# A two-layer hybrid trunk on one core: inputs in one transfer, products of zeros in front, first block ordered by kind, sums and last transfers moved

## The chip, the core and the metric

The kernel runs on one core of a Trainium2 chip. The core has five engines with queues of their own: TensorE (PE, matrix products; its weight loads are listed apart as PEld), VectorE (DVE), ScalarE (ACT), GpSimd (POOL) and SyncE (SP, which here issues the transfers from the chip's memory). The metric is the device time of one execution in microseconds (us); lower is better.

## What is computed

Two layers, each a mixer and a convolutional feed-forward block (FFN), with six modulation vectors made from a conditioning vector `c`, and a norm at the end. Everything is float32, 256 tokens of 1024 channels.

```
def reference(x, c, positions, mod_w, mod_b, norm1_g, norm2_g, w_in, ...):
    for l in range(DEPTH):                      # DEPTH = 2
        mod = c @ mod_w[l] + mod_b[l]
        sh1, sc1, g1, sh2, sc2, g2 = [m[:, None, :] for m in jnp.split(mod, 6, axis=-1)]
        h = _rmsnorm(x, norm1_g[l]) * (1.0 + sc1) + sh1
        x = x + g1 * _mixer(h, positions, w_in[l], ...)
        h = _rmsnorm(x, norm2_g[l]) * (1.0 + sc2) + sh2
        x = x + g2 * _conv_ffn(h, w_up[l], conv_w[l], conv_b[l], w_down[l])
    return _rmsnorm(x, final_g)
```

`_mixer` projects `h` by one wide matrix, runs a sparse attention (an indexer picks 64 keys) and a forgetting attention (a cumulative bias), gates both and projects back. `_conv_ffn` is an up-projection to 2 x 2816 columns, a three-tap convolution along the tokens, `silu(a) * b`, and a down-projection.

## The kernel before, in words

**Tiling.** `x` is kept transposed in SBUF: 8 blocks of 128 channels by 256 tokens (`KT = 8`). Weights come from memory in chunks of about 128 x 1024 float32 into a ring (`raw`). Each chunk is split into a high part `whi` (made by ACT) and a low part `wlo` (made by DVE, raw minus high), activations likewise into `hh`, `hl`; a product is made of three passes: high by high, high by low, low by high (`mm3`, line 121).

**What sets the order.** The program is a list of steps (`add`, line 133), run in order by `run_steps` (line 141); each step names the chunks it needs, and the loader issues their transfers on SP in the order in which the steps list them, as ring slots come free. A scheduler then orders the instructions of each engine by a cost model, except for engines that are pinned (`pin`, line 74): those keep the order in which the code was written.

**The start.** Five transfers are issued first: positions, frequencies, 80 columns of small vectors, and `x` in two halves (lines 244 to 250). `begin` squares `x` and adds the squares; `tables` makes the rotary sines and cosines on DVE and ACT; `masks` makes the masks. `go0` (line 642) then makes the first block of the scale and shift of layer 0 as matrix products of `c` (padded in `cpad`) with a pair of chunks (`mod_mm`, line 615: psM<-raw,cpad), sums the squares over the channels by products with a column of ones (`sum_rows`: psC<-ones), takes the root on POOL (`rstd`), spreads it (psC<-ident,rstd), turns the block's modulation (`mod_fin`: psM<-ident,mods) and makes the block of `h` (`ht` on DVE, `hh` on ACT, `hl` on DVE).

**The blocks.** `go` (line 654) runs over the 8 blocks of channels. Block k multiplies block k of `h` by a 1096-column chunk `wrow[k]` into the accumulators (psA, psB), while the modulation for block k+1 is finished; the modulation products of block k+2 stand at its end, those of block 1 ahead of block 0. A block's modulation is one pair of chunks.

**The other modulation vectors.** They are made on DVE: one chunk of `wmodT` times `c`, summed along the row, one instruction for 128 values (line 357; in the profile CUSTOM_DVE_ANT_0 raw<-raw,cB,vc). There are 80, spread over the stages by the lists `MIXV` and `FFNV` (lines 43, 44): 24 in the mixer of layer 0, 32 in the FFN of layer 0, 16 in the mixer of layer 1, 8 in the FFN of layer 1. In an FFN, `PACE` says how early they are done: all by 1/1.3 of the stage.

**Between stages.** Each norm needs the sum of squares over all channels: squares on ACT, added up on DVE (`sqacc`) or summed one by one on PE. While the root is made, PE runs products whose results nobody reads (`warm`, psM<-cum), in numbers given by `WARMS`. `DSUM = 4` says that at an FFN's end the first four squares are added on DVE. `first_ups` (line 1008) runs the first three up-projections of an FFN block by block as `h` is made.

**The end.** `last` (line 1094) ends the down-projection; the result, scaled by the final gain, is turned back to token rows on PE (psB<-ident,x and psA<-ident,x), multiplied by the root (`yout`), and written out in four transfers of 256 KB on SP (line 1159).

## Time and profile before

| | us |
|---|---|
| median of 3 timed runs | 808.23 (806.09 to 808.28) |
| the profiled execution | 800.14 |
| its span, first to last instruction | 798.3 |
| PE busy in it | 774.5 (97%) |
| DVE busy | 671.2 (84%) |
| ACT busy | 486.8 (61%) |
| mean granted TensorE clock | 0.993 |

The profile is one execution. It was 8.09 us faster than the median of the timed runs; 1.84 us of its time lie outside its span. Rows that begin with two times are from the timeline: start, duration, engine, line, operation, output<-input, shapes, and how many instructions were merged (x8); brackets give the idle time of the engine ahead of it and what ended it. All recorded operations go through one helper, so that every engine shows line L88; the names of the tiles tell them apart. Records of a float32 product with ones or with `cpad` come in twos for each instruction of the program.

### The profile page before, as it was taken

The numbers are of one execution on the slowest core, as the hardware profiler recorded it, in microseconds if no ns is written. First come the engines' busy times: TensorE is split into PE (matmuls) and PEld (weight loads), VectorE is DVE, ScalarE is ACT, GpSimd is POOL, SyncE is SP. The second block draws the span as 40 slices with busy tenths as digits, with TensorE's granted clock in tenths as the row PEclk, the third lists the DMA queues.
The fourth block names the chain that finished last, engine by engine and source line by source line (L and its number), as shares of the span: only waits on it lengthen the run. The fifth ranks groups of instructions, "written<-read, shape, count | busy, mean of one in ns | idle before, by whom it ended". The sixth has DMA issues, their size and how long they took to land.

```text
span 798.3 us, 16595 instructions
## 1 busy us (share of the span) xinstructions
PE 774.5 (97%) x6419; PEld 749.7 (94%) x6419; DVE 671.2 (84%) x1441; ACT 486.8 (61%) x888; POOL 8.0 (1%) x21
## 2 busy tenths in 40 slices
PE   4999999999999999999999999999999999999996
PEld 2899989989999999999989999999999999999996
DVE  6689999998589999998776899997858887877764
ACT  4476566655386665667555756675538666666664
POOL 2000000000000000000000000000000000000000
PEclk9999999999999999999999999999999999999998
DMA  8956777888558999977534577784755766556501
GB/s 324 407 177 204 259 231 255 281 291 289 191 161 285 331 337 334 330 243 225 170 120 122 161 249 248 245 283 150 240 195 156 257 218 211 188 185 186 185 27 54
DMA packets 51919, 179.74 MB, mean 225 GB/s; under 512 B 6272, under 2 KB 6400, under 8 KB 51840
## 3 DMA queue, kind: packets, MB, share of 16 engines
q1 hardware_dynamic: 51840, 178.68, 66.5%
q8 instruction: 50, 0.82, 0.4%
q14 instruction: 29, 0.24, 0.1%
HBM read 177.61 MB, written 1.05 MB: 224 GB/s over the span
## 4 chain that ended last, share of the span: by engine, by line
PE 62%; issue 26%; DVE 8%; ACT 3%; DMA 1%; SPq 0%; POOLq 0%; POOL 0%; DVEq 0%; ACTq 0%
PE psA L88 39%; PE psB L88 19%; DVE wlo L88 2%; PE psM L88 2%; DVE sc L88 1%; PE psC L88 1%; DVE raw L88 1%; ACT whi L88 1%; DMA raw<-wqkf 1%; DMA x<-xT 1%; DVE lg L88 1%; DVE m L88 0%; ACT sq L88 0%; ACT y L88 0%; DVE x L88 0%
## 5 line engine op out<-in xcount | busy, mean ns | idle before, releaser
L88 ACT ACTIVATE whi<-raw 128x1024 fp32r<-128x1024 f32 (+3 forms) x252 | 254.3, 1013 | 140.8 <-PE psA L88 55.8
L88 DVE TENSOR_TENSOR wlo<-raw,whi 128x1024 fp32r<-128x1024 f32 (+3 forms) x252 | 292.1, 1165 | 56.3 <-ACT whi L88 55.4
L88 PE MATMUL psB<-hl,whi 128*128 128x256 f32 x768 | 212.9, 279 | 0.5 <-DVE hl L88 0.5
L88 PE MATMUL psB<-hh,whi 128*128 128x256 f32 x768 | 212.8, 279 | 0.0
L88 PE MATMUL psB<-hh,wlo 128*128 128x256 f32 x768 | 212.6, 278 | 0.0
L88 PEld LDWEIGHTS psB<-hl,whi 128*128 128x128 f32 x768 | 143.7, 188 | 1.0 <-DVE hl L88 0.9
L88 PEld LDWEIGHTS psB<-hh,wlo 128*128 128x128 f32 x768 | 144.0, 188 | 0.0
L88 PEld LDWEIGHTS psB<-hh,whi 128*128 128x128 f32 x768 | 143.6, 188 | 0.2
L88 PE MATMUL psA<-hh,whi 128*128 128x256 f32 x448 | 127.7, 286 | 0.1
L88 PE MATMUL psA<-hl,whi 128*128 128x256 f32 x448 | 125.3, 280 | 0.0
L88 PE MATMUL psA<-hh,wlo 128*128 128x256 f32 x448 | 125.0, 280 | 0.0
L88 DVE CUSTOM_DVE_ANT_0 raw<-raw,cB,vc 128x1024 f32<-128x1024 f32 x80 | 101.6, 1272 | 0.5 <-DMA raw<-wmodT 0.5
L88 PE MATMUL psA<-gl,whi 128*128 128x256 f32 x352 | 97.7, 278 | 0.0
L88 PE MATMUL psA<-gh,whi 128*128 128x256 f32 x352 | 97.4, 279 | 0.3
L88 PE MATMUL psA<-gh,wlo 128*128 128x256 f32 x352 | 97.6, 278 | 0.0
L88 PEld LDWEIGHTS psA<-hh,whi 128*128 128x128 f32 x448 | 84.0, 188 | 2.2 <-issue 1.7
L88 PEld LDWEIGHTS psA<-hl,whi 128*128 128x128 f32 x448 | 84.2, 188 | 0.4
L88 PEld LDWEIGHTS psA<-hh,wlo 128*128 128x128 f32 x448 | 84.1, 188 | 0.0
L88 DVE SCALAR_TENSOR_TENSOR y<-us,vc,y 128x255 f32<-128x255 f32 (+1 forms) x176 | 76.1, 477 | 3.8 <-ACT y L88 3.7
L88 PEld LDWEIGHTS psA<-gh,whi 128*128 128x128 f32 x352 | 65.7, 188 | 0.7 <-ACT gh L88 0.7
L88 PEld LDWEIGHTS psA<-gh,wlo 128*128 128x128 f32 x352 | 66.2, 188 | 0.0
L88 PEld LDWEIGHTS psA<-gl,whi 128*128 128x128 f32 x352 | 66.0, 188 | 0.0
(202 smaller groups left out, 1173.5 us busy)
## 6 DMA issues: line engine op xcount, KB each, us to landing
raw<-wup SPq DMA_DIRECT2D x88, 512.0 KB, 4.3
raw<-wmodT SPq DMA_DIRECT2D x80, 512.0 KB, 4.9
raw<-wdn SPq DMA_DIRECT2D x44, 512.0 KB, 3.9
raw<-wgate SPq DMA_DIRECT2D x32, 512.0 KB, 4.5
raw<-wrow SPq DMA_DIRECT2D x16, 548.0 KB, 6.5
raw<-wbr SPq DMA_DIRECT2D x16, 512.0 KB, 4.8
raw<-wout SPq DMA_DIRECT2D x16, 512.0 KB, 4.0
raw<-wqa SPq DMA_DIRECT2D x16, 320.0 KB, 2.9
```

The costliest lines, as they stand in the source:

```text
L88: r = fn(*a, **kw)
```

## The change

1. **Inputs.** Positions, frequencies and the small vectors are put in front of `x` in one array, and come with it in two transfers on SP (`xs`, 560 KB and 512 KB); `x` becomes a view of it. The zeroing of `tri`, `causal`, `chunked`, `LF` and `cum` goes from DVE to POOL. `cpad` and `vc` get their values by copies on POOL, behind the zeroing of the eight key tiles.
2. **Products of zeros.** `begin` issues 20 products of `cum` (zeros then) on PE; 4 and 10 more stand in `go0`.
3. **First block.** The two sums of squares are no longer added on DVE: PE sums each. `tables` is cut into five steps (`angles`, `turns`, `wholes`, `clamp`, `tables`) which stand with `masks` behind blocks 1 to 6. Block 0 is ordered by kind (all high by high products, then the modulation products of block 1, then all low by high, then all high by low). Chunks are requested one block later, so that `wrow[1]` comes ahead of the modulation pair of block 2.
4. **Sums moved.** The first four sums of vector 3 of layer 1 go from the mixer of layer 1 to the FFN of layer 0 (36 there, 12 in the mixer); `PACE` is 1.15; the mixer's remaining sums begin one step later (`MSTART`).
5. **FFN start.** The gains are made ahead of the last residual instead of behind it; in `first_ups` the further splits of weights begin at block 4 instead of block 1.
6. **Between the FFN of layer 0 and the mixer of layer 1** 3 products without use go ahead of the sums (0 before), and 9 instead of 8 behind them.
7. **The end.** `DSUM` is 2 in layer 1; the sums by products with ones go ahead of the turns, those of blocks 0 to 3 ahead of the last six products. The result leaves in three transfers: 512 KB on SP, 256 KB on ACT's queue, 256 KB on SP.

The diff, cut to its core:

```diff
-WARMS = {"ffn": (4, 8, 10), "mixer": (0, 8, 7)}
+WARMS = {"ffn": (4, 8, 10), "mixer": (3, 9, 7)}
-MIXV = (((0, 2), (0, 3), (0, 4)), ((1, 3), (1, 4)))
-FFNV = (((0, 5), (1, 0), (1, 1), (1, 2)), ((1, 5),))
+MIXV = (((0, 2), (0, 3), (0, 4)), ((1, 3, 4, 8), (1, 4)))
+FFNV = (((0, 5), (1, 0), (1, 1), (1, 2), (1, 3, 0, 4)), ((1, 5),))
-PACE = 1.3
+PACE = 1.15
-DSUM = 4
+DSUM = (4, 2)
+MSTART = (0, 1)
...
-    nc.sync.dma_start(posi, pos)
-    nc.sync.dma_start(ivf, invf)
-    nc.sync.dma_start(vc[:, :V_L + V_CW], vec[:, :V_L + V_CW])
-    for i in range(2):
-        nc.sync.dma_start(x[:, 4 * i:4 * i + 4, :], xT[:, 4 * i:4 * i + 4, :])
+    half = NS + KT * T // 2
+    nc.sync.dma_start(xs[:, :half], xT[:, :half])
+    nc.sync.dma_start(xs[:, half:], xT[:, half:])
...
-    V.memset(f(cum), 0.0)
+    G.memset(f(cum), 0.0)
...
+    def warm(n):
+        for _ in range(n):
+            PE.matmul(HD["fox"][1][:, 0, :], cum[:, :P], cum, start=True, stop=True, skip_group_check=True)
     def begin():
+        pin("V", "PE")
+        clear_keys()
+        HD["fox"] = [halves(bank("B")) for _ in range(2)]
+        HD["sp"] = bank("C")
+        warm(20)
         sq = work.tile([P, 2, 4, T], F32, name="sq0", tag="hl")
+        V.tensor_scalar(ident, jp, 0.0, None, op0=OP.is_equal)
+        G.tensor_copy(cpad[:, :, 0], xs[:, V_C:V_C + KT])
+        G.tensor_copy(vc[:, :V_L + V_CW], xs[:, :V_L + V_CW])
...
-        a, b = ACC["s"]
-        V.tensor_add(a, a, b)
...
             def go0(a, b):
                 pin("V", "A", "PE")
-                start()
+                sum_rows(HD["sp"], ACC["s"][0], True, False)
                 mod_mm(0, 0, a)
-                sp = bank("C")
-                sum_rows(sp, ACC["s"][0], True, True)
+                sum_rows(HD["sp"], ACC["s"][1], False, True)
+                r = rstd(HD["sp"])
                 mod_mm(0, 1, b)
-                r = rstd(sp)
                 state["split_hi"](1)
+                warm(4)
                 mod_fin(0, r)
+                warm(10)
+                start()
...
+            def first(w, a, b):
+                products(w, 0)
+                state["split_hi"](2)
+                mod_both(1, a, b)
+                products(w, 1)
+                state["split"](2)
+                mod_fin(1)
+                products(w, 2)
             def go(k, w, *mc):
-                if k == 0:
-                    mod_both(1, *mc[:2])
-                    mc = mc[2:]
...
+                mod_both(k + 1, *mc)
                 state["split_hi"](2)
...
-                if mc:
-                    mod_both(k + 2, *mc)
             for k in range(KT):
...
+                for fn in {1: [angles], 2: [turns], 3: [wholes], 4: [clamp], 5: [tables], 6: [masks]}.get(k, ()):
+                    add(fn, ahead=0)
...
         def merge(n, w):
             if n == KT - 1:
                 pin(*PINL)
+                gains(l, V_N2, 32)
...
-                if k == 1:
+                if k == 4:
                     state["split"](4)
...
+                if l + 1 == L:
+                    if b == 2:
+                        sum_rows(S["sp"], ACC["a"], True, False)
+                        pin("A", "PE")
+                    while sq and sq[0][0] < 2 * b:
+                        sums(False)
+                    while b < 3 and S["turn"] and S["turn"][0] < 2 * b:
+                        to_rows()
...
+            A.activation(y[:, 0, c], S["tok"][i][0], AF.Copy, scale=r[:, 0:1])
+            V.tensor_scalar(y[:, 1, c], S["tok"][i][1], r[:, 1:2], None, op0=OP.mult)
+            if i == 0:
+                nc.sync.dma_start(rows[:, :, c], y[:, :, c])
+            else:
+                nc.scalar.dma_start(rows[:, 0, c], y[:, 0, c])
+                nc.sync.dma_start(rows[:, 1, c], y[:, 1, c])
```

How the instructions move, as the built programs list them (line, operation, output<-input, shape, and how often in a row). First PE at the program's start, before:

```order
L88 MATMUL psM<-raw_126,cpad 32x256 x4
L88 MATMUL psC<-ones,sqh 128x1 x2
L88 MATMUL psM<-raw_128,cpad 32x256 x4
L88 MATMUL psM<-ident,mods 128x128 x2
L88 MATMUL psC<-ident,rstd 128x128 x2
L88 MATMUL psM<-raw_132,cpad 32x256 x4
L88 MATMUL psM<-raw_134,cpad 32x256 x4
L88 MATMUL psA<-whi,hh 128x320
L88 MATMUL psA<-whi,hh 128x264
L88 MATMUL psA<-whi,hl 128x320
```

The same place on PE, after the change:

```order
L93 MATMUL psB<-cum 128x256 x20
L93 MATMUL psC<-ones,sqh 128x1 x2
L93 MATMUL psM<-raw_119,cpad 32x256 x4
L93 MATMUL psC<-ones,sqh 128x1 x2
L93 MATMUL psM<-raw_121,cpad 32x256 x4
L93 MATMUL psB<-cum 128x256 x4
L93 MATMUL psM<-ident,mods 128x128 x2
L93 MATMUL psC<-ident,rstd 128x128 x2
L93 MATMUL psB<-cum 128x256 x10
L93 MATMUL psA<-whi,hh 128x320
L93 MATMUL psA<-whi,hh 128x264
```

34 products of `cum` are added, the sums of squares now stand on both sides of the first half of the modulation products, and the pair for block 1 (raw_132, raw_134) has left the place ahead of block 0. Next ACT at the start, before:

```order
L88 ACT_TABLE_LOAD
L88 ACTIVATE sq_145<-x 128x1024 x2
L88 ACT_TABLE_LOAD
L88 ACTIVATE ss<-ang 128x2x8
L88 ACTIVATE cc<-nt 128x2x8
L88 COPY mods<-psM 128x256
L88 ACTIVATE whi<-raw 128x1096
L88 ACTIVATE hh<-ht,mod_124 128x256
L88 COPY mods<-psM 128x256
L88 ACTIVATE whi<-raw 128x1096
```

ACT at the start, after the change:

```order
L93 ACT_TABLE_LOAD
L93 ACTIVATE sq_171<-xs 128x1024 x2
L93 COPY mods<-psM 128x256
L93 ACTIVATE whi<-raw 128x1096
L93 ACTIVATE hh<-ht,mod_117 128x256
L93 ACTIVATE whi<-raw 128x1096
L93 COPY mods<-psM 128x256
L93 ACTIVATE hh<-ht,mod_117 128x256
```

The second table load and the sine and cosine have left (they stand five blocks later), and the high part of the second weight chunk (the second `whi`) now stands ahead of the second copy of `mods`. Last, PE at the program's end, before:

```order
L88 MATMUL psA<-gh,wlo 128x256
L88 MATMUL psC<-ones,sqacc 128x1 x2
L88 MATMUL psB<-ident,x 128x128 x2
L88 MATMUL psC<-ones,sq 128x1 x2
L88 MATMUL psA<-ident,x 128x128 x2
L88 MATMUL psC<-ones,sq 128x1 x4
L88 MATMUL psA<-ident,x 128x128 x2
L88 MATMUL psC<-ones,sq 128x1 x2
L88 MATMUL psA<-ident,x 128x128 x4
```

And PE at the end, after the change:

```order
L93 MATMUL psC<-ones,sqacc 128x1 x2
L93 MATMUL psC<-ones,sq 128x1 x4
L93 MATMUL psB<-ident,xs 128x128 x4
L93 MATMUL psA<-gh,whi 128x256
L93 MATMUL psA<-gl,whi 128x256
L93 MATMUL psA<-gh,wlo 128x256
L93 MATMUL psA<-gh,whi 128x256
L93 MATMUL psA<-gl,whi 128x256
L93 MATMUL psA<-gh,wlo 128x256
L93 MATMUL psC<-ones,sq 128x1 x8
L93 MATMUL psA<-ident,xs 128x128 x8
```

Three sums and two turns now stand ahead of the last six products of the down-projection, and the other four sums stand ahead of the last turns instead of between them.

## Rows read from the trace of the kernel before

**Rows 1.** Windows: us, busy us and count by engine, PEclk, DMA share, GB/s.

```profile
0.00:10.00 10.00, 0.58 (x8) 0.23 (x8) 8.40 (x39) 4.40 (x4) 4.55 (x16) 1.00 0.69 235
10.00:20.00 10.00, 8.26 (x53) 5.31 (x46) 5.12 (x19) 3.99 (x8) 0.69 (x1) 1.00 1.03 413
...
240.00:360.00 120.00, 120.00 (x1061) 120.00 (x1060) 120.00 (x195) 76.39 (x115) 0.00 (x0) 1.00 0.89 310
...
400.00:410.00 10.00, 8.23 (x55) 7.82 (x54) 5.08 (x15) 5.02 (x10) 0.69 (x1) 0.83 0.11 44
450.00:540.00 90.00, 89.58 (x697) 84.06 (x696) 88.89 (x280) 59.17 (x144) 0.00 (x0) 1.00 0.74 245
620.00:760.00 140.00, 140.00 (x1191) 140.00 (x1190) 108.97 (x168) 89.18 (x133) 0.00 (x0) 1.00 0.63 203
```

**Rows 2.** Timeline of the start: start us, duration us, engine, what.

```profile
0.74 0.38 SPq L245 DMA_DIRECT2D posi<-pos  x1
...
2.11 0.91 SPq L250 DMA_DIRECT2D x<-xT  x2
...
7.92 1.06 ACT L88 ACTIVATE sq<-x 128x1024 f32<-128x1024 f32 x1 [0.23 <-DMA x<-xT]
...
9.00 1.28 ACT L88 ACT_TABLE_LOAD   x1
...
11.75 1.01 PE L88 MATMUL psC<-ones,sqh 128*128 128x1 f32 x4 [1.25 <-DVE sqh L88]
...
12.70 1.08 PE L88 MATMUL psM<-raw,cpad 128*32 128x256 f32 x8
...
15.74 1.94 PE L88 MATMUL psM<-raw,cpad 128*32 128x256 f32 x16
...
17.60 0.86 PE L88 MATMUL psA<-whi,hh 128*128 128x320 f32 x2
...
18.45 1.12 ACT L88 ACTIVATE whi<-raw 128x1096 fp32r<-128x1096 f32 x1 [0.34 <-DMA raw<-wrow]
...
19.83 0.17 DVE L88 TENSOR_REDUCE modr<-psM 128x2 f32<-128x8 f32 x1 [1.23 <-PE psM L88]
...
20.94 0.51 ACT L88 ACTIVATE hh<-ht,mod 128x256 fp32r<-128x256 f32 x1 [1.37 <-DVE ht L88]
...
21.93 1.07 PE L88 MATMUL psM<-rawg,cpad 128*32 128x256 f32 x16
...
22.93 0.54 PE L88 MATMUL psA<-whi,hh 128*128 128x320 f32 x2
...
27.37 0.54 PE L88 MATMUL psA<-whi,hh 128*128 128x320 f32 x2
```

**Rows 3.** Page, costliest groups: what, count | busy, mean ns | idle before.

```profile
L88 DVE TENSOR_TENSOR wlo<-raw,whi 128x1024 fp32r<-128x1024 f32 (+3 forms) x252 | 292.1, 1165 | 56.3 <-ACT whi L88 55.4
...
L88 DVE CUSTOM_DVE_ANT_0 raw<-raw,cB,vc 128x1024 f32<-128x1024 f32 x80 | 101.6, 1272 | 0.5 <-DMA raw<-wmodT 0.5
```

**Rows 4.** Timeline between the first FFN and the second mixer, PE.

```profile
402.40 0.61 PE L88 MATMUL psC<-ones,sqacc 128*128 128x1 f32 x4 [1.53 <-DVE sqacc L88]
...
405.06 1.92 PE L88 MATMUL psM<-cum 128*128 128x256 f32 x8
```

**Rows 5.** Timeline of the end.

```profile
787.82 1.65 DVE L88 SCALAR_TENSOR_TENSOR x<-psA,mod,x 128x256 f32<-128x256 f32 x4
...
791.92 0.69 POOL L390 TENSOR_TENSOR rstd<-var,mhalf 128x2 f32<-128x2 f32 x1 [195.13 <-DVE var L88]
...
793.42 1.82 SPq L1159 DMA_DIRECT2D out_dram<-yout  x4
```

**Rows 6.** Timeline of the first FFN's start.

```profile
215.31 0.42 ACT L88 ACTIVATE sq<-x 128x256 f32<-128x256 f32 x1 [2.41 <-DVE gain L88]
...
222.65 0.40 PE L88 MATMUL psB<-hh,whi 128*128 128x256 f32 x2
...
223.30 0.39 PE L88 MATMUL psB<-hl,whi 128*128 128x256 f32 x1 [0.25 <-DVE hl L88]
```

More of the change, by code (lines that the diff above doesn't have):

```diff
@@ L301, in clear_keys, with angles @@
                 G.memset(f(t), 0.0)
-    def tables():
+    TB = {}
+    def angles():
         posf = const.tile([P, 2], F32, name="posf")
@@ L315, in tables, with turns @@
         V.tensor_copy(nt, ri)
+        TB["t"] = ang, nt, ri, nh
+    def turns():
+        ang, nt, ri, nh = TB["t"]
         V.tensor_scalar(nh, nt, 1.0 / 4096.0, None, op0=OP.mult)
@@ L359, in mod_columns @@
         return [((lambda raw, n=n: part(n, raw), (wmodT[COLS.index((l, v)), n], D, *kind)), None)
-                for n in range(KT)]
+                for n in range(n0, n1)]
     ACC = {}
@@ L583, in hybrid_trunk, with idle @@
     add(begin, ahead=0)
-    add(tables, ahead=0)
-    add(masks, ahead=0)
     HH = {}
-    def warm(n):
+    def idle(n):
         if n:
@@ L598, in start @@
         def start():
-            HH["h"] = work.tile([P, KT, T], F32R, name="hh"), work.tile([P, KT, T], F32R, name="hl")
+            if "sp" not in HD:
+                HH["h"] = work.tile([P, KT, T], F32R, name="hh"), work.tile([P, KT, T], F32R, name="hl")
+            HD.pop("sp", None)
             S["idx"] = [[bank("A") for _ in range(2)] for _ in range(2)]
-            S["fox"] = [halves(bank("B")) for _ in range(2)]
+            S["fox"] = HD.pop("fox", None) or [halves(bank("B")) for _ in range(2)]
+        late = []
+        if l == 0:
+            for v in MIXV[l]:
+                late += mod_columns(*v)
         def rows(k, w, part):
@@ L685, in second @@
             def second():
-                warm(WARMS["mixer"][1])
+                idle(WARMS["mixer"][1])
                 S["rb"] = rstd_rows(r=S["r"])
-                warm(WARMS["mixer"][2])
+                idle(WARMS["mixer"][2])
                 S["hs"] = h_stream(l, S["rb"], 0, *HH["h"])
@@ L717, in go @@
                     pin()
+            for v in MIXV[l]:
+                late += mod_columns(*v)
             for k in range(KT):
@@ L979, in start @@
             S["sp"] = sp = bank("C")
-            gains(l, V_N2, 32)
-            warm(WARMS["ffn"][0])
+            idle(WARMS["ffn"][0])
             sum_rows(sp, ACC["a"], True, False)
@@ L1071, in ffn @@
         for v in FFNV[l]:
-            nxt += mod_columns(*v, ("s", l + 1))
+            nxt += mod_columns(*v, kind=("s", l + 1))
         total = len(nxt)
@@ L1116, in last @@
                         S["turn"].append(n)
-                while S["turn"] and S["turn"][0] < 2 * b:
-                    to_rows()
+                if l + 1 == L:
[6 more added lines that the diff above has]
+                        to_rows()
         def to_rows():
@@ L1132, in tail @@
         def tail():
-            sum_rows(S["sp"], ACC["a"], True, False)
+            if l + 1 < L:
+                idle(WARMS["mixer"][0])
+                sum_rows(S["sp"], ACC["a"], True, False)
             while S["sq"]:
@@ L1151, in finish @@
         y = work.tile([P, 2, D], F32, name="yout", tag="gt")
+        rows = out.rearrange("(j p) c -> p j c", p=P)
         for i in range(2):
[L1153 to L1159 removed]
+            c = slice(4 * P * i, 4 * P * (i + 1))
+            A.activation(y[:, 0, c], S["tok"][i][0], AF.Copy, scale=r[:, 0:1])
[5 more added lines that the diff above has]
+                nc.sync.dma_start(rows[:, 1, c], y[:, 1, c])
     add(S["tail"])
@@ L1180, in _layout @@
     a["fbias"] = c(np.broadcast_to(i["forget_bias"].reshape(1, -1), (P, L * 8)))
-    a["pos"] = c(i["positions"][0].reshape(2, P).T)
-    a["invf"] = c(np.broadcast_to(np.array(INV_FREQ, np.float32), (P, 8)))
+    xs = np.zeros((P, NS + KT * T), np.float32)
+    m = V_L + V_CW
+    xs[:, :m] = a["vec"][:, :m]
+    xs[:, m:m + 8] = np.array(INV_FREQ, np.float32)
+    xs[:, m + 8:m + 10].view(np.int32)[:] = i["positions"][0].reshape(2, P).T
+    xs[:, NS:] = i["x"][0].T.reshape(KT, P, T).transpose(1, 0, 2).reshape(P, KT * T)
+    a["xT"] = xs
     w = i["w_in"]
```

84 lines of the change are left out of this document (47 added, 37 removed).

## The prediction

> **What bounds the kernel now.** I read the page's busy shares first: PE is busy for 774.5 of 798.3 us, so the time is PE's work plus the few places where PE waits or runs slowly. The windows show where those are [rows 1]: in the first 10 us PE works 0.58 us, in the second 8.26; from 240 to 360 and from 620 to 760 it never stops. Then the timeline at the start, at the two FFN starts, at the change of layers and at the end. In the start the reader is to see two limits: transfers (413 GB/s from 10 to 20 us, DMA share 1.03 [rows 1], and a weight split that waits for its chunk at 18.45 [rows 2]) and a slow PE: 8 records of the same product take 1.08 us at 12.70 and 16 take 1.94 at 15.74, but 16 take 1.07 at 21.93 [rows 2]. PE runs at the lower of its two levels (1.2 GHz) until about 19 us, although the column PEclk shows 1.00 there. From 22.93 on a block takes 27.37 - 22.93 = 4.44 us [rows 2], PE without a gap.
>
> One more thing is needed to read the times. PE's pace in the long stages has two values: 120/1061 = 113.1 ns for a product in the first FFN, 140/1191 = 117.5 in the second, with equal shapes and PEclk 1.00 in both [rows 1]. The stretch at the better pace (240 to 400 us and a little around it, some 1440 products by 4.4 ns) is worth about 6.4 us. The profiled execution took 800.14 us, the timed ones 808.23 in the median, 8.09 more; I take it that the timed ones mostly lack that stretch. The sum below is made on the profiled time and carried to the median as a difference.
>
> **A, the start.** *Transfers.* The three small transfers hold SP from 0.74 to 2.11, where x is issued [rows 2]; x now goes at 0.74, 1.37 us earlier, with the same bytes. I place a chunk by its bytes: 2.35 MB have come at 10.0 us, then 0.413 MB per us [rows 1]; the chunk that ends at 5.36 MB would be there at 17.3 and was split at 18.45 [rows 2], 1.15 later. So a chunk that ends at M megabytes lands after the change at 10 + (M - 2.35)/0.413 + 1.15 - 1.37: the first modulation pair (2.15 MB) at 9.3, the pair of block 1 (3.76) at 13.2, wrow of block 1 (4.32) at 14.5, the pair of block 2 (5.37) at 17.1.
>
> [...]
>
> *Block 0.* The second half of x lands at 7.92 - 1.37 = 6.55 and is squared by 7.6. The sums began 3.83 us behind that square's start, at 11.75; the table load (1.28) has left this stretch [rows 2], so they begin at 9.1 and end near 10.0. From the old sums' end (12.76) to block 0 (17.60) is 4.84, of which the 1.94 of block 1's modulation now stand later: 2.9. Block 0 starts at 10.0 + 2.9 = 12.9; by the pair (9.3 + 4.90 - 1.94) it would be 12.3. I take 12.6; the ten products of zeros in between (1.2 us) lie under this chain.
>
> *Block 1.* A kind of a block costs (4.44 - 1.07 - 0.3)/3 = 1.02. So 12.6, high by high to 13.6, the pair of block 1 to 14.7, second kind to 15.7. The copy of the modulation stands on ACT behind the second whi, which waits for its chunk (14.5 + 1.12 = 15.6), so it ends at 16.0; turn and last kind to 17.3, the pair of block 2 (there at 17.1) to 18.4. Beside it DVE: 14.5 + 1.12, wlo 1.17 [rows 3], then from the reduction to the end of hh 1.62 (19.83 to 21.45 [rows 2]) gives 18.4, and hl a little later. Block 1 starts effectively at 18.8 instead of 22.93: **-4.1**. From there PE takes 4.44 a block and the transfers 1.61/0.413 = 3.9, so PE carries the gain to the end. Bounds: the pair of block 2 forbids more than -5.2; with PE at the lower level all through (0.24 us for a product of cum [rows 4]), 20 products to 7.5, sums and pairs 2 x (1.01 + 1.08) to 11.7, four to 12.7, turns 1.96 to 14.6, ten to 17.0, block 0 and two pairs to 22.5: -0.4.
>
> *What is hidden.* The cut tables put at most 7 steps of about 0.2 us into a block; DVE idles 1.23 ahead of a block's reduction [rows 2], so this costs nothing, and up to 0.3 a block if that idle time goes. The zeroing moved to POOL adds some 1.6 us to its 4.55 [rows 1], the copies at most 0.7 each (the root [rows 5]): cpad is ready near 7.6, before the pair at 9.3; without that cover the excess would go straight onto block 0.
>
> **B, the two FFN starts.** The second block's low product waits: 0.65 us from 222.65 to 223.30 for two products of 0.12, so 0.41 lost [rows 6], behind a wlo that DVE runs in between and that now comes three blocks later. The last square waits for the gains [rows 6], a step of 0.1 to 0.16 which now lies under the last product. **-0.5 each, -1.0**; bounds 0 (the later splits stall PE instead) and -1.4.
>
> **C, the sums moved.** Each costs DVE 1.27 [rows 3]. In the second mixer DVE is busy 88.89 of 90 us, but PE lacks only 0.42 [rows 1]: four sums less give **-0.2** (0 to -0.4). In the first FFN the rate of sums stays (32 x 1.3 = 41.6, 36 x 1.15 = 41.4) and they last longer. DVE is 120 of 120 us busy there [rows 1] and PE still has no gap: **0**; the other end is 4 x 1.27 = +5.1.
>
> **D, between the layers.** PE idles 1.53 ahead of the sums, so three products cost nothing there; behind them PE is at the lower level (8 in 1.92, PEclk 0.83 for the ten us [rows 1, 4]), and a ninth product costs 0.24. If the three keep the level up, eight take 0.94 and the place gains 1.1. Nearest is what is there: **+0.2**.
>
> **E, the end.** The last four residuals start at 787.82, behind an addition of squares that the change drops (two fewer on DVE), and take 1.65 [rows 5]. The root (791.92) follows the last sum, which no longer stands behind turns; four issues of 1.82 in a row become three on two queues [rows 5]. But ACT still has eight squares and eight scalings to do in order. **-1.0**; bounds -0.3 (ACT alone sets the pace) and -1.65.
>
> **Sum.** -4.1 - 1.0 - 0.2 + 0.2 - 1.0 = **-6.1 us**: 794.0 on the profiled execution, 808.23 - 6.1 = **802.1 us** on the median.
>
> **Rivals.** 1. *The products of zeros don't do what they are for*: PE is still at the lower level when it reaches block 0, or falls back while it waits between 7 and 9 us for squares and chunks. For: at 402 a wait of 1.53 and the small sums behind it were followed by the lower level [rows 4]. Against: the chain up to block 1 has a limit of its own (chunk and DVE at 18.4) that hides the first microsecond. Half-way between the bounds, A is -2.2 and the time 804.0. The Trainium skill ("TensorE: Matmul & The Clock Gate", section "HAM oscillation") says that an array that waits goes back to its lower clock; rows 4 agree for this kernel.
> 2. *A better pace in the timed runs*: an FFN falls into the 113.1 ns pace in them. Since the two FFNs of one profile differ [rows 1], it hangs on exact moments, which the change shifts. 802.1 - 6.4 = 795.7.
> 3. *DVE becomes the bound of the first FFN*: it has no idle time left for four sums more, PE waits for the low parts: 802.1 + 5.1 = 807.2. Against it: at the slower pace PE leaves DVE 4% more time than in the profile.
> 4. *Slower*: the timed runs do have the good stretch before (their extra 8 us come from elsewhere), and the change loses it: +6.4 in the first FFN. It decides from the point where the other gains fall below 6.4; with A at -0.4, the rest gives -2.0 and the sum is 808.23 - 2.4 + 6.4 = 812.2.
>
> **Chances.** Forecast 0.56, rival 1 0.20, rival 2 0.09, rival 3 0.08, rival 4 0.07. About 0.3%, 2.4 us, is what a measurement of this kernel can tell from no change. Faster (below 805.8): the forecast, most of rival 1 (0.16) and rival 2: 0.81. Same: the rest of rival 1, rival 3: 0.12. Slower: 0.07. The range leaves out rivals 2 and 4 and holds rival 1: on the low side all terms at their better ends (-5.2 - 1.4 - 0.4 - 1.1 - 1.65 = -9.75: 798.5), less 0.5 for the spread of the runs; on the high side 806.5, which leaves out half of rival 3.
>
> **What would show it.** A right: the PE timeline has block 1's first product at 18.5 to 19.2 and 8 records of the modulation product in about 0.54 us. Rival 1: those 8 take 1.08 and block 1 starts past 20. B: no wait for hl at the first FFN's start. D: psM<-cum near 400 us still at 0.24 each. E: the root follows the last sum directly, with turns behind it, and two queues carry the output. Rival 3: PE waits for wlo between 240 and 380. Rivals 2 and 4: products per window in the FFN, 113 or 117.5 ns. I am wrong if block 1 starts before 17.7 or after 22, or if a stage that I call unchanged, such as the first mixer, moves by over 1 us.

## The result, and the profile after

The changed kernel takes 802.81 us in the median of 17 executions (797.31 to 805.78), the kernel before 807.22 in 17 beside it: a ratio of 0.994, 95% interval 0.9924 to 0.9957. That is 3.5 to 6.1 us less, 4.4 by the medians. 802.1 was forecast. A ratio, here and below, leaves out executions that took over 1.5% longer than the fastest of the same kernel (two of after_again, five of m_sums_old, six of m_pin), which lowers it, while a median takes in all.

The profiled execution of the changed kernel took 799.67 us (span 797.7), that of before 800.14 (798.3): only 0.5 less. To see why, cut both executions at places that each timeline has:

- **start**: up to the first copy of X in mixer 0 (ACT, X<-psA)
- **keys**: from there to the sums over LF (PE, psC<-LF)
- **mixer 0**: on to the root (POOL, rstd<-var) ahead of the first FFN
- **up 0**: root to the first copy of an up-projection (ACT, us<-psB)
- **FFN 0**: on to the end of the last residual (DVE, x<-psA)
- **layers**: on to the first copy of X in mixer 1
- **mixer 1**: on to its root; **up 1**, **FFN 1** (to the last root), **end**: likewise.

Each number is the difference of two start times (for the last residual, its end) in one timeline; a row adds up to its span. The span is known to 0.1 here, so the last stretch is to some 0.05. The kernels below the first two rows are told of in the next section.

| us | start | keys | mixer 0 | up 0 | FFN 0 | layers | mixer 1 | up 1 | FFN 1 | end | span |
|---|---|---|---|---|---|---|---|---|---|---|---|
| before | 50.44 | 43.75 | 122.47 | 12.16 | 175.10 | 27.22 | 164.96 | 12.13 | 183.69 | 6.38 | 798.3 |
| after | 46.04 | 45.30 | 123.10 | 11.64 | 176.00 | 28.80 | 165.13 | 11.63 | 183.29 | 6.77 | 797.7 |
| after_again | 46.27 | 45.31 | 122.45 | 11.64 | 175.99 | 27.66 | 165.21 | 11.63 | 183.74 | 6.80 | 796.7 |
| before_again | 50.33 | 43.76 | 123.69 | 12.15 | 181.13 | 28.64 | 165.34 | 12.15 | 183.44 | 6.47 | 807.1 |
| start_only | 45.86 | 45.30 | 122.40 | 12.00 | 181.12 | 27.48 | 164.24 | 12.14 | 184.19 | 6.57 | 801.3 |
| all_but_start | 50.10 | 43.76 | 121.50 | 11.63 | 181.13 | 27.23 | 165.40 | 11.63 | 183.22 | 6.60 | 802.2 |
| no_zeros | 49.12 | 45.31 | 122.90 | 11.63 | 181.12 | 28.76 | 165.09 | 11.62 | 183.28 | 6.77 | 805.6 |
| masks_early | 45.77 | 43.74 | 123.17 | 11.64 | 181.13 | 27.38 | 164.64 | 11.62 | 177.07 | 6.84 | 793.0 |
| masks_again | 46.26 | 43.76 | 122.20 | 11.64 | 175.99 | 28.74 | 165.21 | 11.63 | 183.27 | 6.90 | 795.6 |
| m_sums_old | 45.62 | 43.75 | 122.39 | 11.64 | 175.11 | 27.50 | 165.86 | 11.63 | 184.07 | 6.83 | 794.4 |
| m_pin | 46.25 | 43.76 | 123.37 | 11.63 | 181.14 | 27.23 | 165.05 | 11.64 | 183.29 | 6.84 | 800.2 |
| m_clock | 45.63 | 43.78 | 123.09 | 11.64 | 181.14 | 27.55 | 165.32 | 11.63 | 183.63 | 6.89 | 800.3 |
| m_tail_old | 46.10 | 43.76 | 124.09 | 11.64 | 181.13 | 27.49 | 165.09 | 11.63 | 177.63 | 6.74 | 795.3 |
| m_inter | 48.54 | 43.75 | 122.23 | 11.64 | 176.00 | 27.95 | 165.36 | 11.63 | 177.38 | 7.52 | 792.0 |

Read the first two rows against each other. The start gives 4.40 and the two FFN starts 0.52 and 0.50. But keys take 1.55 more, mixer 0 0.63, FFN 0 0.90, layers 1.58 and the end 0.39. Which of these belong to the change, and which to the one execution, is what the experiments are for.

**The start.** PE in the timeline of after, to be held against [rows 2]:

```profile
2.72 4.05 PE L93 MATMUL psB<-cum 128*128 128x256 f32 x20 [2.72 <-POOL cum L285]
7.07 0.61 PE L93 MATMUL psC<-ones,sqh 128*128 128x1 f32 x4 [0.29 <-DVE sqh L93]
7.80 0.64 PE L93 MATMUL psM<-raw,cpad 128*32 128x256 f32 x8
...
10.75 1.43 PE L93 MATMUL psB<-cum 128*128 128x256 f32 x10
12.41 0.80 PE L93 MATMUL psA<-whi,hh 128*128 128x320 f32 x4 [0.23 <-ACT hh L93]
...
13.61 1.07 PE L93 MATMUL psM<-raw,cpad 128*32 128x256 f32 x16
...
18.28 0.54 PE L93 MATMUL psA<-whi,hh 128*128 128x320 f32 x2 [0.15 <-ACT hh L93]
18.80 0.53 PE L93 MATMUL psA<-whi,hl 128*128 128x320 f32 x2
...
22.97 0.54 PE L93 MATMUL psA<-whi,hh 128*128 128x320 f32 x2
```

Eight records of the modulation product take 0.64, not 1.08, and sixteen 1.07, not 1.94: PE is at the upper level from about 7 us on. The sums of squares begin at 7.07, block 0 at 12.41, block 1 at 18.28 and block 2 at 22.97. At 4.44 us a block, as before [rows 2], block 2 puts the effective start of block 1 at 18.53, 4.40 ahead of 22.93.

**Keys.** ACT in the timeline, after first:

```profile
46.04 0.68 ACT L93 COPY X<-psA 128x320 f32<-128x320 f32 x2
...
50.38 0.74 ACT L93 CAST kzh<-psB 64x256 fp32r<-64x256 f32 x2 [1.21 <-DVE gl L93]
51.15 1.28 ACT L93 ACT_TABLE_LOAD   x1
...
52.72 0.73 ACT L93 CAST kzh<-psB 64x256 fp32r<-64x256 f32 x2
```

and DVE and PE around it:

```profile
45.36 0.22 DVE L93 TENSOR_SCALAR tri<-jp 128x128 f32<-128x128 int32 x1
45.50 0.22 DVE L93 TENSOR_SCALAR causal<-jp 128x128 f32<-128x128 int32 x1
45.63 0.23 DVE L93 TENSOR_SCALAR e<-ph 128x8 f32<-128x8 int32 x2
45.90 0.17 DVE L93 TENSOR_TENSOR e<-e,e 128x8 f32<-128x8 f32 x1
...
46.10 0.17 DVE L93 CAST pick<-e 128x8 fp32r<-128x8 f32 x1
46.18 1.23 DVE L93 TENSOR_TENSOR wlo<-raw,whi 128x1024 fp32r<-128x1024 f32 x1
...
49.07 0.45 DVE L93 TENSOR_TENSOR rp<-X,cc 128x288 f32<-128x288 f32 x1
```
```profile
54.49 0.63 PE L93 MATMUL psB<-ident,X 128*128 128x128 f32 x4 [0.48 <-DVE kzl L93]
58.57 0.39 PE L93 MATMUL psB<-kzh,qh 128*128 128x256 f32 x1 [1.13 <-DVE ql L93]
```

The masks, which stood in the start before, now stand on DVE among the weight splits, behind which DVE begins to rotate X (rp<-X, at 49.07): 3.03 us behind the first copy of X, where it was 2.20 in before. The second pair of keys is cast only after ACT's table load, and PE waits 0.48 and 1.13.

**FFN 0 and the layers.** Windows of after (columns as in [rows 1]):

```profile
240.00:360.00 120.00, 120.00 (x1061) 120.00 (x1060) 120.00 (x193) 76.74 (x116) 0.00 (x0) 1.00 0.92 325
...
400.00:402.00 2.00, 1.21 (x9) 1.12 (x9) 1.92 (x6) 1.08 (x4) 0.00 (x0) 0.97 0.00 0
402.00:404.00 2.00, 2.00 (x11) 2.00 (x11) 0.15 (x2) 1.59 (x3) 0.00 (x0) 0.50 0.00 0
404.00:406.00 2.00, 2.00 (x10) 2.00 (x11) 0.16 (x1) 0.00 (x0) 0.69 (x1) 0.50 0.00 0
406.00:408.00 2.00, 2.00 (x12) 2.00 (x11) 0.35 (x1) 0.00 (x0) 0.00 (x0) 0.50 0.00 0
408.00:410.00 2.00, 2.00 (x15) 2.00 (x15) 1.81 (x6) 1.84 (x4) 0.00 (x0) 0.83 0.00 0
620.00:760.00 140.00, 140.00 (x1191) 140.00 (x1190) 109.13 (x166) 89.38 (x132) 0.00 (x0) 1.00 0.61 203
```

The paces are those of before: 120/1061 = 113.1 ns a product in the first FFN, 117.5 in the second. The granted clock is down longer than in [rows 1]. A row of 2 us that is at the lower level throughout shows 0.50, so the level is down for twice the part missing from 1.00: 2 x 2 x (0.03 + 0.5 + 0.5 + 0.5 + 0.17) = 6.8 us, against 2 x 10 x 0.17 = 3.4 in [rows 1]. One place inside FFN 0 differs from before, in after's weight loads:

```profile
394.37 0.19 PEld L93 LDWEIGHTS psA<-gl,whi 128*128 128x128 f32 x1 [0.27 <-DVE gl L93]
```

Four us ahead of the end of the products PE waits for a low part (gl) that DVE has just made.

**The end.**

```profile
790.93 0.69 POOL L408 TENSOR_TENSOR rstd<-var,mhalf 128x2 f32<-128x2 f32 x1 [194.23 <-DVE var L93]
...
792.48 0.41 SPq L1227 DMA_DIRECT2D out_dram<-yout  x1
792.95 0.40 ACTq L1229 DMA_DIRECT2D out_dram<-yout  x1
793.09 0.35 SPq L1230 DMA_DIRECT2D out_dram<-yout  x1
```

The root comes 0.99 and the first issue 0.94 earlier than in [rows 5]; the span ends 0.6 earlier. Of the 0.99, FFN 1 with its last sums gives 0.40; 0.50 is its start (up 1) and 0.09 was there before. PE ahead of the root, after first, then the last product of before:

```profile
785.90 0.50 PE L93 MATMUL psC<-ones,sqacc 128*128 128x1 f32 x4
...
787.54 0.36 PE L93 MATMUL psA<-gh,whi 128*128 128x256 f32 x1
...
788.21 0.28 PE L93 MATMUL psA<-gh,wlo 128*128 128x256 f32 x1
```
```profile
787.25 0.28 PE L88 MATMUL psA<-gh,wlo 128*128 128x256 f32 x1
```

From the last product to the root it is 2.72 us in after and 4.66 in before. But the sums and turns that now stand ahead of the last six products hold these up: 1.64 us lie between 785.90 and 787.54.

### The profile page after: what moved, and what is told of

Its sections match the earlier page's. It is cut to its first block, busy times and chain, and to the rows that moved or that the text cites. A ratio compares the mean times of both kernels' runs of the same rounds, so it can differ in the third digit from the quotient of the medians.

```text
span 797.7 us, 16700 instructions
## 1 busy us (share of the span) xinstructions
PE 780.1 (98%) x6469; PEld 756.6 (95%) x6469; DVE 668.8 (84%) x1430; ACT 487.5 (61%) x888; POOL 9.6 (1%) x30
## 4 chain that ended last, share of the span: by engine, by line
PE 56%; issue 27%; DVE 11%; ACT 2%; DMA 2%; SPq 0%; DVEq 0%; POOLq 0%; POOL 0%; ACTq 0%
PE psA L93 36%; PE psB L93 17%; DVE wlo L93 4%; DVE y L93 2%; DVE raw L93 2%; PE psM L93 2%; DMA raw<-wrow 1%; PE psC L93 1%; DVE lg L93 1%; ACT whi L93 1%; DMA raw<-wmodT 1%; ACT y L93 1%; DVE kzl L93 0%; DVE hl L93 0%; DVE xs L93 0%
## 5 line engine op out<-in xcount | busy, mean ns | idle before, releaser
L93 DVE SCALAR_TENSOR_TENSOR y<-us,vc,y 128x254 f32<-128x254 f32 (+1 forms) x176 | 76.9, 479 | 2.9 <-ACT y L93 2.7
```

Source lines behind the costliest of these rows:

```text
L93: r = fn(*a, **kw)
```

## The experiments

All were timed against the kernel before: the first four kernels below in one series, the four from m_clock to m_pin in a second, the last four in a third. The ratios differ from series to series, so the stretches of the table above decide most questions.

| kernel | median (executions) | ratio to before, interval | profiled |
|---|---|---|---|
| start_only | 805.80 (6) | 0.9965 (0.9929 to 1.0001) | 803.27 |
| all_but_start | 804.97 (6) | 0.9975 (0.9951 to 0.9998) | 804.00 |
| no_zeros | 806.80 (6) | 0.9986 (0.9958 to 1.0013) | 807.54 |
| masks_early | 799.98 (6) | 0.9903 (0.9875 to 0.9930) | 794.75 |
| m_clock | 800.55 (12) | 0.9919 (0.9888 to 0.9950) | 802.01 |
| m_tail_old | 799.97 (11) | 0.9921 (0.9893 to 0.9950) | 796.96 |
| m_sums_old | 800.74 (12) | 0.9878 (0.9833 to 0.9923) | 796.15 |
| m_pin | 801.23 (12) | 0.9881 (0.9839 to 0.9924) | 801.97 |
| after_again | 800.54 (6) | 0.9878 (0.9836 to 0.9919) | 798.63 |
| masks_again | 797.23 (4) | 0.9878 (0.9863 to 0.9894) | 797.31 |
| m_inter | 800.21 (6) | 0.9891 (0.9854 to 0.9929) | 793.87 |
| before_again | 806.95 (12) | 0.9979 (0.9956 to 1.0003) | 808.86 |

**Which half carries it.** *start_only* is the changed kernel with all but the start put back, *all_but_start* the kernel before with all but the start.

> The kernel before with the new start alone (one input tile, products of zeros, block 0 by kind, the tables cut up); sums, first FFN starts, products between the layers and the end are the old ones. Theory (the start carries the gain, and part of it is lost behind it): block 1 starts at 18.3 to 18.9 and the first evacuation of mixer 0 at 46.0, 4.4 us ahead of before; the masks still stand ahead of that evacuation, so about 1.6 is lost again by 60 us and the first branch product comes 2.5 to 3.1 ahead of before's 169.05. Time 803.7 to 804.7, 2.5 to 3.5 below before. Rival (the medians differ because the timed runs of the changed kernel reach the quicker pace of PE more often, for reasons outside the start): the time stays within 1 us of before, 806.2 to 808.2.

> The changed kernel with the start of before. Theory (start carries the gain): what is left is two FFN starts at -0.5 each, the end at 0 to -0.4, the three products between the layers at +1.1 (the clock falls before the small sums and not behind them) and the longer sums in the first FFN at 0 to +0.9: the time is 806.2 to 808.2, no change. Rival (pace or the moved sums carry it): 803 to 805, at least half of the gain of the whole change.

The start takes 45.86 alone and 50.10 without it: the 4.4 are the start's. Keys cost 45.30 with the new start and 43.76 without. The FFN starts take 11.63 with the change and 12.00 and 12.14 without. The times alone confirm neither theory. start_only gains 1.2 us by the medians, between the two; all_but_start gains 2.0, and its 804.97 lies in the rival's range. With six executions each, and intervals that reach to 1.0001 and 0.9998, that decides nothing; the stretches show what each half does.

**The products of zeros.**

```
-        warm(20)
...
-                warm(4)
...
-                warm(10)
```

> The changed kernel without the products of zeros in front (20, 4 and 10 of them left out), all else equal. Theory (they raise the clock, and that pays for block 0): the sums and the pairs of the start run at the lower level, a pair in 1.9 to 2.2 us and not 1.07, a kind of block 0 in about 2 us, block 1 starts at 21 to 22.5 and not 18.8; time 2.2 to 3.7 above the changed kernel. Rival (the chunks and DVE set block 1 anyway): block 1 at 18.8 to 19.5, time within 0.7 us of the changed kernel.

```profile
8.05 1.08 PE L93 MATMUL psM<-raw,cpad 128*32 128x256 f32 x8
...
16.36 1.88 PE L93 MATMUL psM<-raw,cpad 128*32 128x256 f32 x16
...
21.60 0.54 PE L93 MATMUL psA<-whi,hh 128*128 128x320 f32 x2
```

Eight records take 1.08 and sixteen 1.88 again, block 1 begins at 21.60, the start takes 49.12, as the theory said. The 34 products of zeros are worth 3.1 of the start's 4.4 us. The other 1.3 (inputs, order of block 0, cut tables) were not tried apart.

**The masks.** Six DVE steps, moved from behind block 6 into the start, where DVE waits 4.11 us for the first square (in after):

```profile
5.71 0.69 DVE L93 TENSOR_TENSOR sq<-sq 128x512 f32<-128x512 f32 x1 [4.11 <-ACT sq L93]
```

```
         V.tensor_scalar(ident, jp, 0.0, None, op0=OP.is_equal)
+        masks()
...
-                for fn in {1: [angles], 2: [turns], 3: [wholes], 4: [clamp], 5: [tables], 6: [masks]}.get(k, ()):
+                for fn in {1: [angles], 2: [turns], 3: [wholes], 4: [clamp], 5: [tables]}.get(k, ()):
```

> The changed kernel with its six mask steps on DVE moved from behind block 6 into the idle stretch at the start (behind the identity, 1.6 us). Theory (the masks ahead of mixer 0's evacuation cost the 1.6 us that went missing there): the rotation starts 2.2 us behind the first copy of X and not 3.0, the keys of both pairs are cast before the table load on ACT, the last kzl ends 6.1 us behind that copy and not 8.3, PE's waits of 0.48 and 1.13 at 54 to 58 us go, and all that follows is 1.5 to 2.0 earlier; time 1.0 to 2.0 below the changed kernel. Rival (the loss is a wait for weights that would come anyway, or a later wait takes it back): the first branch product moves by under 0.5, time within 0.7.

ACT in masks_early, then PE:

```profile
45.77 0.67 ACT L93 COPY X<-psA 128x320 f32<-128x320 f32 x2
...
49.28 1.51 ACT L93 CAST kzh<-psB 64x256 fp32r<-64x256 f32 x4 [0.38 <-DVE gl L93]
50.81 1.28 ACT L93 ACT_TABLE_LOAD   x1
```
```profile
89.51 0.73 PE L93 MATMUL psC<-LF,tri 128*128 128x8 f32 x6
```

The sums over LF begin at 89.51, 43.74 behind the copy. Keys take 45.30 or 45.31 in all four profiles with the masks behind block 6, and 43.74 to 43.78 in all ten others: the place of the masks costs 1.55 us. In masks_early DVE begins to rotate X at 47.96, 2.19 behind the first copy, 0.84 sooner than in after, all four casts come ahead of the table load, and PE's waits of 0.48 and 1.13 are gone. By these rows 0.84 is DVE's delay and the rest the order of casts and table load on ACT, which changes with it; the two were not tried apart. All kernels whose names begin with m_ are made from this one.

**The clock between the layers.**

```
-WARMS = {"ffn": (4, 8, 10), "mixer": (3, 9, 7)}
+WARMS = {"ffn": (4, 8, 10), "mixer": (14, 9, 7)}
```

> The version with the masks at the start, and 14 products of zeros ahead of the small sums between the layers, not 3; nothing else. They take about 1.6 us at 113 to 118 ns each and fill the wait of 0.86 to 1.44 us there. Theory (the level falls because PE waits ahead of the sums): the granted clock stays 1.00 through the place, the nine products behind the sums take 1.0 us and not 2.0, and mixer 1's first evacuation comes 1.0 to 1.7 us earlier, counted from the last residual of the first FFN; time 1.0 to 1.7 lower than the version it is made from, for the same pace. Rival (the small sums with one column, or the wait for the root, bring the level down anyway): the clock shows 0.50 for some 3.4 us as in the other traces, and nothing moves by over 0.3.

```profile
402.00:404.00 2.00, 2.00 (x19) 2.00 (x18) 1.51 (x4) 0.42 (x1) 0.00 (x0) 1.00 0.23 94
404.00:406.00 2.00, 1.95 (x19) 1.86 (x18) 1.36 (x5) 1.82 (x5) 0.00 (x0) 1.00 0.00 0
406.00:408.00 2.00, 2.00 (x13) 2.00 (x13) 0.16 (x1) 0.80 (x1) 0.69 (x1) 0.63 0.00 0
408.00:410.00 2.00, 2.00 (x11) 2.00 (x11) 0.42 (x2) 0.00 (x0) 0.00 (x0) 0.52 0.00 0
```

The rival holds. PE is busy for 7.95 of 8 us (second column) and the level falls at about 406.5 all the same, behind 20 records of sums with one column. The layers take 27.55, no gain. So the fall needs no wait ahead of the sums, contrary to my reading of [rows 4]. The Trainium skill ("TensorE: Matmul & The Clock Gate", section "HAM oscillation") tells of falls after waits; here one came without a wait.

**Sums put back.**

```
-MIXV = (((0, 2), (0, 3), (0, 4)), ((1, 3, 4, 8), (1, 4)))
-FFNV = (((0, 5), (1, 0), (1, 1), (1, 2), (1, 3, 0, 4)), ((1, 5),))
+MIXV = (((0, 2), (0, 3), (0, 4)), ((1, 3), (1, 4)))
+FFNV = (((0, 5), (1, 0), (1, 1), (1, 2)), ((1, 5),))
...
-PACE = 1.15
+PACE = 1.3
...
-MSTART = (0, 1)
+MSTART = (0, 0)
```

> The version with the masks at the start, and the sums of the modulation where they were: all of layer 1's third column vector in the second mixer, the pace of the sums in the first FFN at 1.3, the second mixer's sums from the first attention unit on. Theory (the move cost the first FFN nothing and freed DVE a little in the second mixer): at equal pace of PE the first FFN takes 0 to 0.4 us longer than with the move and the second mixer 0 to 0.4; together 0 to +0.8. Rival (the move makes DVE the bound of the first FFN): it is 0.5 us or more shorter without the move, and PE waits for no low part of g near its end.

This profile has the quicker pace in the first FFN, as before, after, after_again, masks_again and m_inter have. With the old sums FFN 0 takes 175.10 and 175.11, with the moved ones 176.00, 175.99, 175.99 and 176.00: +0.9 from the move and its PACE. The four with +0.9 have PE's wait for gl (394.37 in after); the two without have none, and from that wait on a product takes 117.8 ns and not 113.3. At the slower pace it is 181.12 or 181.13 with the old sums (before_again, start_only) and 181.12 to 181.14 with the moved ones: nothing. The rival is right at the one pace and wrong at the other. Mixer 1 takes 165.86 here, against 164.64 to 165.40 with the moved sums; but before (164.96), before_again (165.34) and start_only (164.24) have the old ones too, so no gain is shown.

**DVE's order in the last branch step.**

```
             zh, zl = S["z"]
+            if n == KT - 1:
+                pin("V")
...
+            if n == 1:
+                pin()
```

> The version with the masks at the start, and DVE's order fixed in the last branch step, so that the low part of z comes ahead of the weight splits that the next step asks for (it also places two sums of the modulation and these splits behind it). Theory (what is lost between the first branch product and the root of the first FFN is PE's wait for that low part, 0.3 to 0.5 us at the first merge product): that wait goes, and the stretch takes 47.6 us and not 48.0. Rival (the splits that now come later make PE wait instead): the stretch takes 48.0 or more, with a wait for wlo in the merge.

Of that stretch, from the first branch product to the root, m_pin needs 47.46, and 47.46 again in mixer 1, which the edit changes too. But seven other profiles have 47.61 without the edit, before and after_again among them, before_again has 49.01 and all_but_start 46.87, the least of all: the loss comes and goes with the execution. Inconclusive, at best 0.15.

**The end.**

```
-            if i == 0:
-                nc.sync.dma_start(rows[:, :, c], y[:, :, c])
-            else:
-                nc.scalar.dma_start(rows[:, 0, c], y[:, 0, c])
-                nc.sync.dma_start(rows[:, 1, c], y[:, 1, c])
+            for j in range(2):
+                nc.sync.dma_start(rows[:, j, c], y[:, j, c])
```

> The version with the masks at the start, and the last transfers as before: four of 256 KB on SP's queue, not 512 KB on SP, 256 KB on ACT's and 256 KB on SP. Theory (the new transfers gave back what the earlier root had won): from the root to the end it takes 6.4 us as before and not 6.8, so the end comes 0.4 earlier; the first transfer waits for two scalings less. Rival (the bytes set it, 1.05 MB at about 380 GB/s are 2.8 us, or four issues on one queue cost what they cost before): 6.7 to 7.2 us from the root to the end, no gain or a loss of up to 0.4.

6.74 from the root to the end: the old transfers do not bring 6.38 back. The arrangement of the transfers neither gains nor loses more than 0.1. From the first issue to the last landing it is 4.1 us with the old transfers (before, before_again, start_only, m_tail_old) and 4.2 with the new ones in halves. What follows the last landing is 0.8 to 0.9 in the three profiles with the start of before and 1.0 to 1.2 in all others, start_only included, whose end is the old one and takes 6.57. So of the extra 0.2 to 0.4 some 0.15 comes with the transfers, and 0.2 to 0.35 in the kernels with the new start; why the start should lengthen what follows the last landing stays open.

**Once more.** The changed kernel, the one with the masks early and the kernel before, in one series.

> The changed kernel once more, for a second profile and for times beside the next ones. In its first profile it gained only 0.5 us on the kernel before, with PE's two paces set equal, though the medians differ by 4.4. Theory (that execution was an unlucky one: the granted clock was down for 6.8 us between the layers and not 3.4, and at the quicker pace PE caught up with DVE at the end of the first FFN): now the stretch from the last residual of layer 0 to mixer 1's first evacuation takes 27.2 to 27.5 us and not 28.8, the first FFN 181.1 and not 182.3 at equal pace, and the whole is 2.5 to 3.5 below before. Lost for good, in both profiles: 1.55 us between mixer 0's first evacuation and its decay sums (45.3 against 43.75). Rival (the change itself costs these stretches, and the median owes its gain to a luckier pace): the whole is again within 1 us of before at equal pace.

> The version with the masks at the start once more, on the same chip as the changed kernel. Theory: evacuation to decay sums in mixer 0 43.75 us and not 45.3, the time 1.0 to 2.0 below the changed kernel. Rival (weights come later then, and PE waits for them further on): the same 43.75, but the whole of mixer 0 within 0.5 of the changed kernel, and the time within 0.7.

> The kernel before once more. Theory (the two paces of PE are drawn anew in each execution, at a wait of PE, and hold until the next): the first FFN is at 117.8 ns a product in this profile or at 113.3, and where it is 117.8 the execution takes 806 to 808 us; with the paces set equal each stage is within 0.3 us of the first profile, mixer 0's and the layers' change included. Rival (the pace belongs to the program): the first FFN is at 113.3 ns again and the profiled execution takes 800 us.

The layers take 27.66 in after_again, mixer 0 122.45, while keys stay at 45.31. The long fall is a matter of the execution, not of the change: it comes in after, no_zeros, masks_again and before_again (28.64 to 28.80), the short one in the ten others (27.22 to 27.95). The profiled time, 798.63, is 1.5 below before's 800.14 at the same pace in FFN 0, where 2.5 to 3.5 had been expected: between the theory and the rival. The part of the theory on FFN 0 failed: the pace was the quicker one again, and 0.9 went again.

before_again answers on the pace:

```profile
240.00:360.00 120.00, 120.00 (x1021) 120.00 (x1021) 120.00 (x193) 78.57 (x117) 0.00 (x0) 1.00 0.90 309
```

The same program, 120/1021 = 117.5 ns a product and not 113.1, and 808.86 us and not 800.14. FFN 0 takes 181.13, not 175.10. So the pace does not belong to the program. The rest of that theory did not hold: mixer 0 takes 1.22 and the layers 1.42 more than in before, where 0.3 had been allowed.

masks_again keeps its 43.76, and its times lie 3.3 below after_again; of that 1.55 is the masks', and the rest cannot be told from the pace with so few executions.

**Wide products between the small sums, output in quarters.**

```
             while S["sq"]:
+                if l + 1 < L:
+                    idle(2)
                 sums(len(S["sq"]) == 1)
...
-        for i in range(2):
-            c = slice(4 * P * i, 4 * P * (i + 1))
...
+        for i in range(4):
+            c, d = slice(2 * P * i, 2 * P * (i + 1)), slice(i % 2 * 2 * P, (i % 2 + 1) * 2 * P)
...
+            nc.sync.dma_start(rows[:, :, c], y[:, :, c])
```

> The version with the masks at the start, with two products of zeros (256 columns) ahead of each of the four small sums of squares between the layers, and the output scaled and sent in four quarters of 256 columns (both halves of the tokens in one transfer), all on SP's queue. Theory for the clock (the sums, products with one column, bring it down, since it fell although PE was never idle with 14 products ahead of them): with wide products between them the level stays up, no row at 0.50 between the layers, the nine products behind take 1.0 us; the eight cost 0.9, so the place gains 0.3 to 0.8. Rival (the wait for the root brings it down): it falls for 3.4 us as ever, and the place loses 0.5 to 0.9. For the end: the first transfer is issued 0.4 earlier behind the root; if the bytes set the rest, from the root to the end it takes 6.4 us, not 6.8; if the smaller rows make the transfers slower, 6.8 or more.

The clock falls again for some 3.4 us and the layers take 27.95: 0.3 to 0.6 lost. Here PE waited 1.45 ahead of the sums; that wait and the sums' single columns were each taken away, not both together. The end takes 7.52, with the first issue 1.29 behind the root and not 1.55. The last landing comes 6.5 behind the root, against 5.6 in m_tail_old, which also issues four transfers on SP: rows of half the length, or both halves of the tokens in one transfer, cost more than the earlier issue gives.

This profile shows something else. Its start is masks_again's, instruction for instruction, but:

```profile
8.17 1.08 PE L93 MATMUL psM<-raw,cpad 128*32 128x256 f32 x8
...
13.29 2.34 PE L93 MATMUL psB<-cum 128*128 128x256 f32 x10
...
21.01 0.54 PE L93 MATMUL psA<-whi,hh 128*128 128x320 f32 x2
```

PE is still at the lower level in the ten products at 13.29 (0.23 each, 0.14 in after), in spite of those ahead of them, and block 1 begins at 21.01. Of the ten profiles with the products of zeros, nine have a start of 45.6 to 46.3 and this one has 48.54.

## Why the prediction was right, point by point

**A, the start (-4.1).** Right in size: the start is 4.40 and 4.06 shorter (after against before, again against again), and block 1 starts effectively at 18.53, where 18.8 was forecast. From block 0 on the reasons hold too: block 0 at 12.41 (12.6 forecast), the pair of block 1 at 13.61, and block 1 waits for hh, the last step of DVE and ACT ahead of it; its first product, at 18.28, comes 0.2 ahead of the sign that I had named. Ahead of block 0 two errors nearly cancel, which is luck: the sums begin at 7.07 and not 9.1, and from there to block 0 it is 5.3 us and not 3.8. Rival 1 is real but rare: m_inter is its case, and no_zeros its price, 3.1. Two figures of the prediction there are slips: the -2.2 of rival 1 lies half-way between -0.4 and the forecast, not between the bounds, and the bound of -0.4 counts block 0 and its two pairs at the upper level, though it says lower all through.

**What is hidden (0).** This step failed, and it is the largest error. I counted the cut tables as some 0.2 us a step under DVE's idle 1.23 in a block [rows 2]. That holds for the steps in the blocks: all that block 1 gained is still there at the first copy of X. The masks come last, where DVE runs weight splits in a row up to the rotation of X, and the order of casts and table load on ACT changes with the delay: +1.55. The cover that I named ends where the blocks end. I had written that I am wrong if the first mixer moves by over 1 us; by that sign this step is wrong, though the time came out right.

**B, the FFN starts (-0.5 each).** Right: -0.52 and -0.50 in after, the same in every kernel with the change, and PE's wait for hl [rows 6] is gone in each of them. The part that I gave to the gains does not show: from the first branch product to the root it is 47.61 in before and in after_again.

**C, the sums (-0.2).** At the slower pace nothing in FFN 0, as said. At the quicker one +0.9, where I had put 0 because PE had no gap there: near the end DVE is too late with gl, and PE waits. That is rival 3 on a small scale; what I had said against it, that the slower pace leaves DVE more time, is true of the slower pace alone. The gain in mixer 1 does not show in after (+0.2).

**D, the layers (+0.2).** Not to be told from zero: with the short fall the kernels with three products take 27.23 to 27.66, and the old arrangement 27.22 (before) and 27.48 (start_only). Right that three do not hold the level up, though filling the wait does not either. The long fall (+1.1 to +1.4) was missing from my cases.

**E, the end (-1.0).** This step failed as well: with the old end FFN 1 and end together take 189.9 to 190.8 (before, before_again, start_only), with the new one, at the same pace, 189.8 to 190.9. Behind the last product the forecast was right and more, 2.72 to the root for 4.66. What I left out is that PE never waits ahead of the last six products, so that sums and turns put there hold these products up: from the thirteenth product from the end to the last it is 3.51 in every profile with the new end and 2.04 with the old. From that product to the root 0.24 is left (6.22 for 6.46, all_but_start and before_again, where the granted clock stays up until the last sum), and the stretch behind the root takes 0.2 to 0.4 back. Where the level falls during the last sums the root comes up to 0.8 later (m_sums_old: eight records of the sums in 1.84 us, 1.06 in after); that is most of the spread of FFN 1. And I had taken the issues for the limit of the output: the transfers, and what follows them, are.

**The sum.** In the terms that repeat: -4.2 (start) + 1.55 (keys) - 1.02 (FFN starts) + 0 (FFN 0) + 0.1 (layers) + 0 (FFN 1 and end) = -3.6 in place of -6.1; -2.7 at the quicker pace in FFN 0. The first pair of profiles has that pace, and on top of it the long fall (1.4) and 0.6 in mixer 0, so that 0.6 of the span was left.

**The carry to the median** was the right step: the profile of before lay in a minority. Of all 92 executions of before, 12 took under 804.5 us (median 801.17) and 80 more (807.35); of 23 of the changed kernel, 7 took under 800.5 (797.70) and 16 more (802.94). Like with like, the change gives 3.5 in the quicker group and 4.4 in the other, where the repeating terms say 2.7 and 3.6. The groups are told by their times; which pace an execution had is seen in the profiles alone. So some 0.8 us are not accounted for; they may lie in stretches that vary, mixer 0 above all. That 802.1 stood so near to 802.81 is partly luck: 2.5 us of the forecast gain were not there, 0.8 came from elsewhere, and 1.0 from the kernel before itself, whose median was 808.23 in three executions and 807.22 in the 17 beside the changed kernel.

**A version that beats both** is masks_early: 798.22 us in the median of ten executions in two series, 802.74 for the changed kernel's 23 (797.23 and 800.54 in the one series that has both). The part of it that is shown is 1.55 us.

## What to carry to other kernels

When work is taken out of a waiting start, ask for each step where it lands; the last one lands outside the cover that was counted for the others. Cut two executions at the same landmarks before explaining a difference of medians: stretches that repeat to 0.05 us can be priced from two profiles, the others cannot. When work is moved ahead of something, ask whether the engine waits there: PE did not wait ahead of the last six products, so nothing was won by it. Look at a second profile before pricing a change of half a per cent.

## What the runs showed of the hardware

- **PE has two paces at the same granted clock.** From start to start of 256-column products it is 113.3 or 117.8 ns (the counts of the windows, which take in the products at both edges, give 113.1 and 117.5). Where it was followed, it changes at a restart of PE (the first product of an FFN, of the merge, of the down-projection) and holds until the next; in after, after_again, masks_again and m_inter the quicker pace of FFN 0 ends at the wait for gl. Of 28 FFNs in 14 profiles nine have the quicker one, worth 6.0 us in the first (181.13 to 175.10) and 6.2 in the second (183.3 to 177.07). What decides it stays open. DVE's load does not by itself: FFN 0 has either pace with DVE busy for 120 of 120 us, and the second FFN of masks_early has the quicker one with DVE at 80% (112.36 of 140 us in this window of it), where after, at 78%, has the slower.

```profile
620.00:760.00 140.00, 140.00 (x1238) 140.00 (x1237) 112.36 (x174) 94.16 (x140) 0.00 (x0) 1.00 0.65 206
```

- **The lower level lasts some 3.4 or 6.8 us between the layers**, in one program the one or the other (before and before_again), with 1.1 to 1.4 us between them.
- **POOL's small copies** took 0.19 and 0.24 us, where I had bounded them by the root's 0.69.
